# Packed 64x64 scores and a state per chunk in a gated linear attention, and its small steps moved from GpSimd to VectorE, in a fused encoder layer

## The chip, the cores and the metric

The kernel runs on one core of one Trainium2 chip and computes one whole layer for one sequence of 1024 frames and 1024 channels. The metric is the device time of one execution in microseconds (us). Each time is a median over runs of the compiled kernel; the profile is one more execution, taken apart by the chip's profiler. PE is TensorE (matmuls), DVE is VectorE, ACT is ScalarE, POOL is GpSimd, SP is SyncE, which issues the DMAs.

## What is computed

The layer is `x = LN1(alpha*x + gate1*m)`, `x = LN2(alpha*x + gate2*f)`; `f` is a feed-forward part of width 4096 and `m` mixes the tokens: `u @ w_in` is cut into heads, four heads of retention (with rotary positions) and four of gated linear attention (GLA), each normalized and gated, and `w_out` joins them. The change concerns the heads. The core of GLA, with chunks of 64 frames, keys of 64 and values of 128 channels a head, `b` being summed log gates:

```python
def step(state, inp):
    qi, ki, vi, lai = inp
    b = jnp.cumsum(lai, axis=1)
    decay = jnp.exp(-jnp.abs(b[:, :, None] - b[:, None, :]))
    A = jnp.einsum('bthd,bshd,btshd->bhts', qi, ki, decay)
    o = jnp.einsum('bhts,bshe->bthe', A, vi)
    o = o + jnp.einsum('bthd,bhde->bthe', qi * jnp.exp(b), state)
    b_last = b[:, -1]
    new_state = jnp.exp(b_last)[..., None] * state + jnp.einsum(
        'bshd,bshe->bhde', ki * jnp.exp(b_last[:, None] - b), vi)
    return new_state, o
```

Inside a chunk the decay differs for each channel and is symmetric in t and s, so A is not one matrix product.

## The kernel before

**Projections.** A product in float32 is made of three in fp32r: each operand is split into a high part, a cast on ScalarE, and a low part, source minus high part (`split`, L205 and L206; the low part goes to GpSimd unless the call names an engine), and `mm3` (L211 to L213) multiplies high by high, high by low and low by high. The contraction over 1024 channels runs in 8 blocks of 128, the frames in two halves `h` of 512. `load_w` brings a block of weights by DMA and splits it (`wh`, `wl`); `take` keeps one or two of the next weights loaded ahead. `modulate` makes the normalized input `u` and its parts `uh`, `ul`. `feature_major` puts channels on partitions (queries and keys), `values` puts frames there.

**GLA.** `gla(blk, h)` is called four times, for two pairs of heads (`blk`) and two halves of the frames; two heads of 64 channels lie one above the other on 128 partitions. A level of size u (32, 16, 8, 4, 2, 1) covers those pairs (t, s) of a chunk that lie in the two halves of one block of 2u frames: there |b_t - b_s| is a sum of two differences to the block's middle, and the scores are one product of decayed queries and keys. For each level GpSimd forms the differences `E` (L562, L563), ScalarE their exponentials (L564), VectorE the products `qe` and `ke` (L566, L567), TensorE the scores (L544, 128 frames by 128 frames for each of 2 heads and 4 blocks of frames; the profile shows each such matmul as two), and VectorE lays them over the sum `am` under the level's mask (`overlay`, L552). Two sets come ahead of the levels: the first chunk of each 128 frames against the second (`kB`, `qB`, copied under a mask, L554), and the diagonal (`k`, `q`, laid over under the identity).

**State.** It steps over 128 frames, so GpSimd makes `qI`, `kI` and `dt` (L576, L577, L580), which carry the first chunk's decay. TensorE transposes `kI` (L583) and forms the updates `up` (L593), VectorE makes the states one after another (L598, L600), TensorE reads them (L611) and adds the scores times the values (L617), and the heads are normalized (L621 to L626).

**Retention.** `retention_qk` turns the projections by the rotary tables: three products on VectorE (L647 to L649), their sum `t1` and the scaled queries `qd` on GpSimd (L650, L654); `retention` begins with scores at L663.

**Beside it.** `ada_sum` (L236, L238) sums the blocks of the conditioning vector's weights into `acc` on VectorE, and `load_out` splits the output weights (L800, `ol` on both engines).

**The order of work.** The program names its steps in the order of L751 to L786; the tile framework's scheduler then puts each engine's instructions into one order, by its own estimates of when operands and buffers are ready. Each engine works its row in order. Around the change:

```python
d = gla_decays(0, 0)
gla_qk(1)
ada(ada_row(2560, g1[1]))
gla(0, 0, gv0, *d)
d = gla_decays(0, 1)
gv1 = values(("gv", 1))
```

Of the kernel before, what the change touches and what calls it, by code (L numbers as in the profile page):

```python
# [16 lines left out]
P = 128  # L17
# [24 lines left out]
C_M64 = C_QD + 512  # L42
C_LV = C_M64 + 128
LEVELS = (32, 16, 8, 4, 2, 1)
C_KD = C_LV + 128 * len(LEVELS)
# [6 lines left out]
def shape_constants():  # L52
# [27 lines left out]
def layer_kernel(ctx: ExitStack, tc, x, c, w_ada, b_ada, w_in, ret_norm_w, gla_gate_w, gla_gate_b,  # L80
# [269 lines left out]
    def load_w(ranges, kk):  # L350
# [3 lines left out]
        for k in range(0, NK, kk):  # L354
# [6 lines left out]
            split(w, th, tl)  # L361
# [152 lines left out]
    def gla_decays(blk, h):  # L514
# [11 lines left out]
        G.tensor_tensor(out=ek.rearrange("p (n u) -> p n u", u=CHUNK),  # L526
# [7 lines left out]
    def gla(blk, h, gv, q, k, b, eb, qB, kB):  # L534
        am = [S(n="am"), S(n="am")]

        def scores(ka, qa, put):

            heads = [slice(64 * hd, 64 * hd + 64) for hd in range(2)]
            tiles = [slice(j * P, (j + 1) * P) for j in range(4)]  # L540
# [7 lines left out]
        def cmask(o):  # L548
            return table(o).unsqueeze(1).broadcast_to([P, 4, P])

        def overlay(o):
            return lambda a, ps: V.copy_predicated(out=a, mask=cmask(o).bitcast(U32), data=ps)  # L552

        scores(kB, qB, lambda a, ps: V.tensor_tensor(out=a, in0=ps, in1=cmask(C_M64), op=ALU.mult))  # L554
        scores(k, q, overlay(C_ID))
        for n, u in enumerate(LEVELS):
# [5 lines left out]
            G.tensor_tensor(out=ev[:, :, :u], in0=ref, in1=bv[:, :, :u], op=ALU.subtract)  # L562
            G.tensor_tensor(out=ev[:, :, u:], in0=bv[:, :, u:], in1=ref, op=ALU.subtract)  # L563
# [4 lines left out]
            scores(ke, qe, overlay(C_LV + P * n))  # L568


        eb4 = eb.rearrange("p (j c u) -> p j c u", c=2, u=CHUNK)
        qI, kI = S(n="qI"), S(n="kI")
        for src, dst, c0 in ((qB, qI, 0), (kB, kI, 1)):
            s4 = src.rearrange("p (j c u) -> p j c u", c=2, u=CHUNK)
            d4 = dst.rearrange("p (j c u) -> p j c u", c=2, u=CHUNK)
            G.tensor_copy(out=d4[:, :, c0, :], in_=s4[:, :, c0, :])  # L576
            G.tensor_tensor(out=d4[:, :, 1 - c0, :], in0=s4[:, :, 1 - c0, :],  # L577
                            in1=eb4[:, :, c0, CHUNK - 1:CHUNK].broadcast_to([P, 4, CHUNK]), op=ALU.mult)
        dt = small(4, "gdt", bufs=4)
        G.tensor_tensor(out=dt, in0=eb4[:, :, 0, CHUNK - 1], in1=eb4[:, :, 1, CHUNK - 1], op=ALU.mult)  # L580
        kp = mxt()
        for j in range(4):
            T.transpose(out=kp[:, j * P:(j + 1) * P], in_=kI[:, j * P:(j + 1) * P], identity=ident)  # L583
# [11 lines left out]
        states = S((P, 4, P), n="states")  # L595
        for j in steps:
            if before[j] is None:
                V.tensor_copy(out=states[:, j, :], in_=up[:, j, :])  # L598
            else:
                V.scalar_tensor_tensor(out=states[:, j, :], in0=before[j], scalar=dt[:, j:j + 1], in1=up[:, j, :],  # L600
                                       op0=ALU.mult, op1=ALU.add)
            before.append(states[:, j, :])
# [3 lines left out]
        with_state = [j for j in range(4) if before[j] is not None]  # L606
# [33 lines left out]
    def retention_qk(hd):  # L640
        res = [[], []]
        for key in ("rq", "rk"):
            pss = feature_major((key, hd))
            for h, ps in enumerate(pss):
# [5 lines left out]
                G.tensor_tensor(out=t1, in0=t1, in1=t2, op=ALU.add)  # L650
# [627 lines left out]
```

## Time and profile before

| | |
|---|---|
| Median of 3 runs | 1276.38 us (1275.5 to 1276.91) |
| The profiled execution: time | 1275.61 us |
| its span in the profile | 1273.8 us, 18210 instructions |
| PE busy | 1187.6 us, 93% |
| DVE busy | 965.2 us, 76% |
| ACT busy | 496.4 us, 39% |
| POOL busy | 301.0 us, 24% |

The span runs from the first to the last instruction; 1.8 us of the execution's time lie outside it. A busy share is a mean over stages that differ: the rows further down are taken by stretches. 0 to 128 us are the conditioning, the first norm and the first projections; 128 to 352 us hold GLA with the projections around it; up to 512 us run retention, the gates and the beginning of the output projection; then follow the rest of it and the feed-forward part. The granted clock is TensorE's, as a share of 2.4 GHz.

### The profile page before, as it was taken

Reading aid. Unit: us, or ns where it says so; the run is one execution under the profiler, and the core shown is the slowest. Engines: PE = TensorE matmul, PEld = TensorE weight load, DVE = VectorE, ACT = ScalarE, POOL = GpSimd, SP = SyncE. Lnnn points to the kernel's source line nnn. Section 1 sums busy time; section 2 is a strip of 40 time slices with the busy share of each in tenths; the row PEclk is TensorE's granted clock in tenths of the full one; section 3 lists DMA queues with packets and bytes.
Section 4 is the critical chain, followed back from the end, with each engine's and each line's share of the span. In section 5 each row is a group of like instructions: output and inputs, shape, how many; then the busy total and the mean of one; then the engine's idle time right before and its main releaser. Section 6 shows DMA issues by size and latency. Waiting matters only on the chain. (4 is left out here: it accounts for less than half of the span.)

```text
span 1273.8 us, 18210 instructions
## 1 busy us (share of the span) xinstructions
PE 1187.6 (93%) x6491; PEld 993.7 (78%) x6491; DVE 965.2 (76%) x1778; ACT 496.4 (39%) x879; POOL 301.0 (24%) x253
## 2 busy tenths in 40 slices
PE   4899899879899989999998999999999999999995
PEld 1588789667887979988886887888887788888784
DVE  6884876798757585379889978876657786897996
ACT  4424332122121323223475446665655443441222
POOL 1333442463324423000000000000002222242336
PEclk9899989889999999999999999999999999999998
DMA  9685220100011032227124768676464455458632
GB/s 313 207 269 200 83 59 5 38 25 26 9 50 34 21 105 65 77 77 246 53 93 149 245 203 300 232 248 207 149 220 164 142 190 186 134 192 284 233 124 100
DMA packets 124124, 183.31 MB, mean 144 GB/s; under 512 B 12337, under 2 KB 52482, under 8 KB 124034
## 3 DMA queue, kind: packets, MB, share of 16 engines
q1 hardware_dynamic: 124034, 182.16, 43.0%
q8 instruction: 51, 0.84, 0.3%
q14 instruction: 39, 0.32, 0.1%
HBM read 137.02 MB, written 45.09 MB: 143 GB/s over the span
## 5 line engine op out<-in xcount | busy, mean ns | idle before, releaser
L211 PE MATMUL pj<-wh,uh 128*128 128x256 f32 (+1 forms) x512 | 146.5, 287 | 0.3 <-ACT wh L205 0.3
L212 PE MATMUL pj<-wl,uh 128*128 128x256 f32 (+1 forms) x512 | 145.9, 285 | 0.3 <-POOL wl L206 0.3
L213 PE MATMUL pj<-wh,ul 128*128 128x256 f32 (+1 forms) x512 | 146.1, 286 | 0.0
L206 POOL TENSOR_TENSOR al<-rh,ah 128x512 fp32r<-128x512 f32 x17 | 26.7, 1571 | 468.0 <-ACT w1h L205 399.4
L206 POOL TENSOR_TENSOR wl<-st,wh 128x512 fp32r<-128x512 f32 (+1 forms) x60 | 78.2, 1320 | 190.3 <-ACT wh L205 118.9
L211 PE MATMUL pj<-uhp,w1h 128*128 128x512 f32 x256 | 100.2, 393 | 2.0 <-ACT w1h L205 1.1
L211 PE MATMUL pj<-bh,ah 128*128 128x512 f32 x256 | 99.8, 391 | 1.5 <-DVE qv L181 0.8
L212 PE MATMUL pj<-ulp,w1h 128*128 128x512 f32 x256 | 100.0, 391 | 0.0
L213 PE MATMUL pj<-uhp,w1l 128*128 128x512 f32 x256 | 99.9, 391 | 0.0
L212 PE MATMUL pj<-bl,ah 128*128 128x512 f32 x256 | 99.6, 389 | 0.0
L213 PE MATMUL pj<-bh,al 128*128 128x512 f32 x256 | 99.6, 389 | 0.0
L211 PEld LDWEIGHTS pj<-wh,uh 128*128 128x128 f32 x512 | 98.0, 192 | 1.3 <-ACT wh L205 0.7
L212 PEld LDWEIGHTS pj<-wl,uh 128*128 128x128 f32 x512 | 98.2, 192 | 0.9 <-POOL wl L206 0.5
L213 PEld LDWEIGHTS pj<-wh,ul 128*128 128x128 f32 x512 | 98.2, 192 | 0.4 <-issue 0.2
L211 PE MATMUL mx<-uhp,w1h 128*128 128x512 f32 x192 | 75.1, 392 | 2.7 <-ACT w1h L205 2.7
L211 PE MATMUL mx<-bh,ah 128*128 128x512 f32 x192 | 75.4, 394 | 2.1 <-ACT bh L205 1.2
L212 PE MATMUL mx<-bl,ah 128*128 128x512 f32 x192 | 75.6, 394 | 1.1 <-POOL bl L206 0.9
L213 PE MATMUL mx<-bh,al 128*128 128x512 f32 x192 | 75.5, 393 | 0.0
L213 PE MATMUL mx<-uhp,w1l 128*128 128x512 f32 x192 | 75.3, 393 | 0.0
L212 PE MATMUL mx<-ulp,w1h 128*128 128x512 f32 x192 | 75.3, 392 | 0.0
L212 PE MATMUL pj<-ul,wh 128*128 128x512 f32 x176 | 71.1, 406 | 4.3 <-DVE ul L206 2.6
L211 PE MATMUL pj<-uh,wh 128*128 128x512 f32 x176 | 72.0, 411 | 2.7 <-ACT uh L205 2.7
(266 smaller groups left out, 3014.5 us busy)
## 6 DMA issues: line engine op xcount, KB each, us to landing
raw<-in_w_ff SPq DMA_DIRECT2D x140, 256.0 KB, 4.2
ada<-in_w_ada SPq DMA_DIRECT2D x96, 256.0 KB, 5.4
rh<-hid SPq DMA_DIRECT2D x84, 256.0 KB, 3.7
hid<-c SPq DMA_DIRECT2D x54, 256.0 KB, 2.3
st<-in_w_in SPq DMA_DIRECT2D x52, 256.0 KB, 3.0
hid<-m SPq DMA_DIRECT2D x30, 256.0 KB, 2.2
hid<-kl SPq DMA_DIRECT2D x28, 256.0 KB, 3.1
hid<-kh SPq DMA_DIRECT2D x28, 256.0 KB, 2.7
```

Source lines behind the costliest of these rows:

```text
L206: (lo_eng or G).tensor_tensor(out=lo, in0=src, in1=hi.bitcast(F32), op=ALU.subtract)
L211: T.matmul(ps, lhsT=lh, rhs=rh, start=first, stop=False, skip_group_check=partial)
L212: T.matmul(ps, lhsT=lh, rhs=rl, start=False, stop=False, skip_group_check=partial)
L213: T.matmul(ps, lhsT=ll, rhs=rh, start=False, stop=last, skip_group_check=partial)
```

## The change

It has three parts. **Scores:** queries meet keys of their own chunk alone, as blocks of 64 by 64 that lie on four quarters of the PE array (two heads as row halves, two chunks as column halves), so `am` is half as wide, each mask has 64 columns, and the set of `qB` against `kB` is gone; the diagonal set is copied whole by ScalarE ahead of the levels. **State:** it steps over 64 frames, 8 (or 7) steps a call, with the last column of each chunk's `eb` as its decay; `qI`, `kI` and `dt` are gone; updates, state reads and the products of `am` and values are cut into more and smaller matmuls. **Engines:** whatever GpSimd computed in projections and mixing (`E`, `ek`, `wl`, half of `ul` and of `ol`, the rotary sum and `qd`) is written on VectorE. Lines of the program after the change are lower by one up to `gla` and differ a little within it (scores L549, overlay L556, `E` L565 and L566, `qe` and `ke` L569 and L570, `acc` L237, low part L205).

```diff
 modulate:
-        split(u, uh[k][h], ul[k][h], lo_eng=(V, G)[h])
+        split(u, uh[k][h], ul[k][h], lo_eng=V)
 load_w:
-            split(w, th, tl)
+            split(w, th, tl, lo_eng=V)
 gla_decays:
-        G.tensor_tensor(out=ek.rearrange("p (n u) -> p n u", u=CHUNK),
+        V.tensor_tensor(out=ek.rearrange("p (n u) -> p n u", u=CHUNK),
...
 gla:
-        am = [S(n="am"), S(n="am")]
+        am = S((P, 2, 4, CHUNK), n="am")
+        rows = [slice(CHUNK * i, CHUNK * i + CHUNK) for i in range(2)]
...
             pss = [mxt(), mxt()]
-            for o in tiles:
+            for j in range(4):
                 for hd in range(2):
-                    T.matmul(pss[hd][:, o], lhsT=ka[heads[hd], o], rhs=qa[heads[hd], o], start=True, stop=True)
+                    for ch in range(2):
+                        o = cols(2 * j + ch)
+                        T.matmul(pss[hd][rows[ch], cols(j)], lhsT=ka[rows[hd], o], rhs=qa[rows[hd], o], start=True,
+                                 stop=True)
             for hd in range(2):
-                put(am[hd].rearrange("p (j t) -> p j t", t=P), pss[hd].rearrange("p (j t) -> p j t", t=P))
+                put(am[:, hd], pss[hd][:, :4 * CHUNK].rearrange("p (j t) -> p j t", t=CHUNK))
...
-        scores(kB, qB, lambda a, ps: V.tensor_tensor(out=a, in0=ps, in1=cmask(C_M64), op=ALU.mult))
-        scores(k, q, overlay(C_ID))
+        scores(k, q, lambda a, ps: A.copy(out=a, in_=ps))
...
-            G.tensor_tensor(out=ev[:, :, :u], in0=ref, in1=bv[:, :, :u], op=ALU.subtract)
-            G.tensor_tensor(out=ev[:, :, u:], in0=bv[:, :, u:], in1=ref, op=ALU.subtract)
+            V.tensor_tensor(out=ev[:, :, :u], in0=ref, in1=bv[:, :, :u], op=ALU.subtract)
+            V.tensor_tensor(out=ev[:, :, u:], in0=bv[:, :, u:], in1=ref, op=ALU.subtract)
...
-        steps = range(4 if h == 0 else 3)
+        steps = range(8 if h == 0 else 7)
...
-        up = mxt((P, 4, P))
-        for j in steps:
-            vt = gv[2 * h + j // 2][:, j % 2, :]
+        up = [mxt((P, 4, P)), mxt((P, 4, P))]
+        for n in steps:
+            j, ch = n // 2, n % 2
             for hd in range(2):
-                T.matmul(up[64 * hd:64 * hd + 64, j, :], lhsT=kt[:, j * P + 64 * hd:j * P + 64 * hd + 64],
-                         rhs=vt[:, hd * P:(hd + 1) * P], start=True, stop=True)
+                T.matmul(up[ch][rows[hd], j, :], lhsT=kt[rows[ch], j * P + CHUNK * hd:j * P + CHUNK * hd + CHUNK],
+                         rhs=ve(j, hd, ch), start=True, stop=True)
...
-        for j in with_state:
-            o = slice(j * P, (j + 1) * P)
+        for n in with_state:
             for hd in range(2):
-                r = slice(64 * hd, 64 * hd + 64)
-                T.matmul(op[hd][:, j, :], lhsT=qI[r, o], rhs=before[j][r, :], start=j == with_state[0], stop=False,
-                         skip_group_check=True)
+                T.matmul(op[hd][rows[n % 2], n // 2, :], lhsT=qB[rows[hd], cols(n)], rhs=before[n][rows[hd], :],
+                         start=n in with_state[:2], stop=False, skip_group_check=True)
         for hd in range(2):
             for j in range(4):
-                o = slice(j * P, (j + 1) * P)
-                vt = gv[2 * h + j // 2][:, j % 2, :]
-                T.matmul(op[hd][:, j, :], lhsT=am[hd][:, o], rhs=vt[:, hd * P:(hd + 1) * P], start=False, stop=j == 3,
-                         skip_group_check=True)
+                for t in range(0, CHUNK, 32):
+                    for ch in range(2):
+                        T.matmul(op[hd][CHUNK * ch + t:CHUNK * ch + t + 32, j, :], lhsT=am[rows[ch], hd, j, t:t + 32],
+                                 rhs=ve(j, hd, ch), start=False, stop=j == 3, skip_group_check=True)
 retention_qk:
-                G.tensor_tensor(out=t1, in0=t1, in1=t2, op=ALU.add)
+                V.tensor_tensor(out=t1, in0=t1, in1=t2, op=ALU.add)
...
 load_out:
-                split(w, oh[k][q], ol[k][q], lo_eng=(G, V)[q])
+                split(w, oh[k][q], ol[k][q], lo_eng=V)
```

`qd` is written with V in place of G in the same way. The scheduler puts the work of the rest into other places than before; three show how.

**First place: PE, in the first call of gla(), between the scores of its first two levels.** `mx_1313`, `mx_1314` (`mx_1308`, `mx_1309` after) are the scores of level 32, `pj` a projection. Before:

```order
L544 MATMUL mx_1313<-qe_1309,ke_1310 128x128
L544 MATMUL mx_1314<-qe_1309,ke_1310 128x128
L544 MATMUL mx_1333<-qe_1329,ke_1330 128x128
L544 MATMUL mx_1334<-qe_1329,ke_1330 128x128
...
L212 MATMUL pj_1528<-wl_1150,uh_278 128x256
L213 MATMUL pj_1528<-wh_1149,ul_279 128x256
```

After:

```order
L549 MATMUL mx_1308<-qe_1304,ke_1305 64x64 x2
L549 MATMUL mx_1309<-qe_1304,ke_1305 64x64 x2
L212 MATMUL pj_1609<-wh_1161,ul_622 128x256
L210 MATMUL pj_1609<-wh_1161,uh_627 128x256
L211 MATMUL pj_1609<-wl_1162,uh_627 128x256
L212 MATMUL pj_1609<-wh_1161,ul_628 128x256
...
L549 MATMUL mx_1336<-qe_1332,ke_1333 64x64 x2
L549 MATMUL mx_1337<-qe_1332,ke_1333 64x64 x2
```

Before, the scores of the next level follow at once; after, 18 matmuls of a projection stand between the two levels. From the first to the last score matmul of the four calls there are 65, 65, 31 and 36 projection matmuls in the row before, and 129, 129, 68 and 96 after.

**Second place: DVE, in the same call, the same two levels.** `acc` belongs to the conditioning. Before:

```order
L566 TENSOR_TENSOR qe_1309<-gqk_694,E_1305 128x512
L567 TENSOR_TENSOR ke_1310<-gqk_778,E_1305 128x512
L238 SCALAR_TENSOR_TENSOR acc_2708<-ada_2698,keep,acc_2708 128x512
L566 TENSOR_TENSOR qe_1329<-gqk_694,E_1325 128x512
L567 TENSOR_TENSOR ke_1330<-gqk_778,E_1325 128x512
L238 SCALAR_TENSOR_TENSOR acc_2708<-ada_2700,keep,acc_2708 128x512
L552 COPY_PREDICATED am_1279<-cst_77,mx_1313 128x512
L552 COPY_PREDICATED am_1280<-cst_77,mx_1314 128x512
```

After:

```order
L569 TENSOR_TENSOR qe_1332<-gqk_694,E_1328 128x512
L570 TENSOR_TENSOR ke_1333<-gqk_778,E_1328 128x512
L565 TENSOR_TENSOR E_1356<-b_1108 128x32x8
L566 TENSOR_TENSOR E_1356<-b_1108 128x32x8
L237 SCALAR_TENSOR_TENSOR acc_2951<-ada_2943,keep,acc_2951 128x512
L556 COPY_PREDICATED am_1279<-cst_77,mx_1336 128x256
L556 COPY_PREDICATED am_1279<-cst_77,mx_1337 128x256
L569 TENSOR_TENSOR qe_1360<-gqk_694,E_1356 128x512
```

The two halves of the next level's `E` now stand behind `ke`, and the overlays are half as wide.

**Third place: DVE, behind the last level of the first call,** where the heads' norm is made (L172 to L174 are steps of the reciprocal root, `go` the normalized output) and the next call's decays begin. Before, and then after:

```order
L173 SCALAR_TENSOR_TENSOR rt_386_1498<-ry_385_1497 128x4
L174 TENSOR_TENSOR rt_386_1498<-rt_386_1498,rv_384_1496 128x4
L175 SCALAR_TENSOR_TENSOR grs_1494<-rt_386_1498,ry_385_1497 128x4
L626 TENSOR_TENSOR go_1510<-mx_1455,grs_1494 128x512
L530 TENSOR_TENSOR qB_1524<-gqk_696,eb_1518 128x512
```

```order
L172 SCALAR_TENSOR_TENSOR rt_382_1579<-ry_381_1578 128x4
L205 TENSOR_TENSOR wl_2175<-st_2172,wh_2174 128x512
L173 TENSOR_TENSOR rt_382_1579<-rt_382_1579,rv_380_1577 128x4
L205 TENSOR_TENSOR wl_2181<-st_2178,wh_2180 128x512
L174 SCALAR_TENSOR_TENSOR grs_1575<-rt_382_1579,ry_381_1578 128x4
L205 TENSOR_TENSOR wl_2760<-st_2757,wh_2759 128x512
L622 TENSOR_TENSOR go_1591<-mx_1504,grs_1575 128x512
L525 TENSOR_TENSOR ek_1602<-b_1598 128x512
L529 TENSOR_TENSOR qB_1605<-gqk_696,eb_1599 128x512
```

The low parts `wl` of the next weights have come in among these small steps, and `ek` ahead of `qB`.

## Rows read from the trace of the kernel before

**Rows 1.** Windows: us, busy us and instructions by engine, granted clock, DMA share, GB/s
```profile
0.00:128.00 128.00, 103.17 (x514) 74.80 (x515) 88.64 (x147) 53.27 (x97) 40.50 (x39) 0.96 0.74 246
128.00:352.00 224.00, 194.18 (x1569) 172.49 (x1568) 173.04 (x341) 53.28 (x91) 95.77 (x101) 0.94 0.12 35
352.00:512.00 160.00, 150.26 (x1072) 139.32 (x1072) 104.89 (x249) 42.34 (x73) 57.66 (x40) 1.00 0.20 57
```

**Rows 2.** Waits of PE, 128 to 352 us: total us, times, longest
```profile
PE mx L544 <- DVE ke L567: 24.8, 17, 8.2
```

**Rows 3.** Windows of the four bodies of gla(), their sum (102.5 us)
```profile
sum 102.50, PE 77.49 PEld 66.81 DVE 94.79 ACT 19.05 POOL 67.01; mean PE 19.37 PEld 16.70 DVE 23.70 ACT 4.76 POOL 16.75
```

**Rows 4.** Timeline, 266 to 285 us: start, us, engine, line, operation
```profile
...
267.72 1.59 POOL L654 TENSOR_TENSOR qd<-t,cst 128x512 f32<-128x512 f32 x1
268.20 1.66 DVE L648 TENSOR_TENSOR t<-p,rope 64x512 f32<-64x512 f32 x1
...
269.88 0.68 DVE L649 TENSOR_TENSOR t<-p,rope 64x512 f32<-64x512 f32 x1
...
```

**Rows 5.** Groups of DVE, 128 to 352 us: count, busy us, mean ns, idle before
```profile
L552 DVE COPY_PREDICATED am<-cst,mx 128x512 f32<-128x512 uint32 x48 | 31.7, 724 | 2.4 <-PE mx L544 2.2
L566 DVE TENSOR_TENSOR qe<-gqk,E 128x512 f32<-128x512 f32 x24 | 19.9, 831 | 4.2 <-ACT E L564 4.2
L567 DVE TENSOR_TENSOR ke<-gqk,E 128x512 f32<-128x512 f32 x24 | 19.1, 797 | 0.0
L238 DVE SCALAR_TENSOR_TENSOR acc<-ada,keep,acc 128x512 f32<-128x512 f32 x14 | 13.5, 967 | 0.1
L648 DVE TENSOR_TENSOR t<-p,rope 64x512 f32<-64x512 f32 x8 | 11.4, 1420 | 0.1
L647 DVE TENSOR_TENSOR t<-p,rope 128x512 f32<-128x512 f32 x8 | 9.8, 1228 | 0.9 <-ACT p L646 0.7
L649 DVE TENSOR_TENSOR t<-p,rope 64x512 f32<-64x512 f32 x8 | 8.5, 1059 | 0.1
...
L600 DVE SCALAR_TENSOR_TENSOR states<-states,gdt,mx 128x128 f32<-128x128 f32 x12 | 4.2, 348 | 1.7 <-PE mx L593 1.4
...
L531 DVE TENSOR_TENSOR kB<-gqk,ek 128x512 f32<-128x512 f32 x4 | 2.7, 685 | 0.0
```

**Rows 6.** Group of DVE, 352 to 512 us, a form of 256 columns
```profile
L736 DVE TENSOR_TENSOR mix<-sg,ro 128x256 f32<-128x256 f32 x6 | 2.3, 422 | 1.7 <-POOL ol L206 1.5
```

**Rows 7.** Groups of POOL, 128 to 352 us
```profile
L206 POOL TENSOR_TENSOR wl<-st,wh 128x512 fp32r<-128x512 f32 x17 | 23.1, 1374 | 58.4 <-ACT wh L205 47.8 <-PE pj L212 10.5
L562 POOL TENSOR_TENSOR E<-b 128x256 f32<-128x256 f32 x24 | 19.5, 814 | 12.6 <-DVE ke L567 9.8 <-DVE acc L238 2.7
...
L650 POOL TENSOR_TENSOR t<-t,t 128x512 f32<-128x512 f32 x8 | 12.6, 1574 | 8.8 <-DVE t L649 8.8
```

**Rows 8.** Timeline, 176 to 186 and 155.5 to 160.2 us
```profile
176.03 0.97 PEld L544 LDWEIGHTS mx<-qB,kB 64*128 64x128 f32 x16 [0.76 <-issue]
176.92 0.98 PEld L544 LDWEIGHTS mx<-gqk,gqk 64*128 64x128 f32 x16
...
178.24 0.28 PE L212 MATMUL pj<-wl,uh 128*128 128x256 f32 x1
178.36 0.28 PE L213 MATMUL pj<-wh,ul 128*128 128x256 f32 x1
...
155.58 1.09 PE L593 MATMUL mx<-v,kt 128*64 128x128 f32 x16
...
158.26 2.05 PE L617 MATMUL mx<-v,am 128*128 128x128 f32 x16
```

**Rows 9.** Waits of PE, 0 to 512 us
```profile
PE mx L663 <- POOL t L650: 3.1, 1, 3.1
...
PE pj L211 <- ACT uh L205: 2.7, 1, 2.7
PE pj L212 <- DVE ul L206: 2.6, 1, 2.6
```

More of the change, by code (lines that the diff above doesn't have):

```diff
@@ L41 @@
 C_QD = C_DEC + 512
[L42 to L43 removed]
+C_LV = C_QD + 512
 LEVELS = (32, 16, 8, 4, 2, 1)
[L45 removed]
+C_KD = C_LV + CHUNK * len(LEVELS)
 C_N = C_KD + 4
@@ L534, in gla, with cols @@
     def gla(blk, h, gv, q, k, b, eb, qB, kB):
-        am = [S(n="am"), S(n="am")]
+        am = S((P, 2, 4, CHUNK), n="am")
+        rows = [slice(CHUNK * i, CHUNK * i + CHUNK) for i in range(2)]
+        def cols(n):
+            return slice(CHUNK * n, CHUNK * n + CHUNK)
         def scores(ka, qa, put):
-            heads = [slice(64 * hd, 64 * hd + 64) for hd in range(2)]
-            tiles = [slice(j * P, (j + 1) * P) for j in range(4)]
             pss = [mxt(), mxt()]
-            for o in tiles:
+            for j in range(4):
                 for hd in range(2):
-                    T.matmul(pss[hd][:, o], lhsT=ka[heads[hd], o], rhs=qa[heads[hd], o], start=True, stop=True)
+                    for ch in range(2):
+                        o = cols(2 * j + ch)
+                        T.matmul(pss[hd][rows[ch], cols(j)], lhsT=ka[rows[hd], o], rhs=qa[rows[hd], o], start=True,
+                                 stop=True)
             for hd in range(2):
-                put(am[hd].rearrange("p (j t) -> p j t", t=P), pss[hd].rearrange("p (j t) -> p j t", t=P))
-        def cmask(o):
-            return table(o).unsqueeze(1).broadcast_to([P, 4, P])
+                put(am[:, hd], pss[hd][:, :4 * CHUNK].rearrange("p (j t) -> p j t", t=CHUNK))
         def overlay(o):
-            return lambda a, ps: V.copy_predicated(out=a, mask=cmask(o).bitcast(U32), data=ps)
-        scores(kB, qB, lambda a, ps: V.tensor_tensor(out=a, in0=ps, in1=cmask(C_M64), op=ALU.mult))
-        scores(k, q, overlay(C_ID))
+            m = table(o, CHUNK).unsqueeze(1).broadcast_to([P, 4, CHUNK]).bitcast(U32)
+            return lambda a, ps: V.copy_predicated(out=a, mask=m, data=ps)
+        scores(k, q, lambda a, ps: A.copy(out=a, in_=ps))
         for n, u in enumerate(LEVELS):
@@ L567, in gla @@
             V.tensor_tensor(out=ke, in0=k, in1=e, op=ALU.mult)
[L568 to L578, printed above, removed]
@@ L579, in gla, with ve @@
-        dt = small(4, "gdt", bufs=4)
-        G.tensor_tensor(out=dt, in0=eb4[:, :, 0, CHUNK - 1], in1=eb4[:, :, 1, CHUNK - 1], op=ALU.mult)
+            scores(ke, qe, overlay(C_LV + CHUNK * n))
         kp = mxt()
         for j in range(4):
-            T.transpose(out=kp[:, j * P:(j + 1) * P], in_=kI[:, j * P:(j + 1) * P], identity=ident)
+            T.transpose(out=kp[:, j * P:(j + 1) * P], in_=kB[:, j * P:(j + 1) * P], identity=ident)
         kt = S(n="kt")
         A.copy(out=kt, in_=kp)
-        steps = range(4 if h == 0 else 3)
+        def ve(j, hd, ch):
+            return gv[2 * h + j // 2][rows[ch], j % 2, hd * P:(hd + 1) * P]
@@ L603, in gla @@
+        states = [S((P, 4, P), n="states"), S((P, 4, P), n="states")]
+        for n in steps:
+            new, u = states[n // 4][:, n % 4, :], up[n % 2][:, n // 2, :]
+            if before[n] is None:
+                V.tensor_copy(out=new, in_=u)
+            else:
+                V.scalar_tensor_tensor(out=new, in0=before[n], scalar=eb[:, CHUNK * n + CHUNK - 1:CHUNK * n + CHUNK],
+                                       in1=u, op0=ALU.mult, op1=ALU.add)
+            before.append(new)
         gstate[blk] = before[-1]
@@ L604, in gla @@
         op = [mxt((P, 4, P)), mxt((P, 4, P))]
-        with_state = [j for j in range(4) if before[j] is not None]
-        for j in with_state:
-            o = slice(j * P, (j + 1) * P)
+        with_state = [n for n in range(8) if before[n] is not None]
+        for n in with_state:
             for hd in range(2):
-                r = slice(64 * hd, 64 * hd + 64)
-                T.matmul(op[hd][:, j, :], lhsT=qI[r, o], rhs=before[j][r, :], start=j == with_state[0], stop=False,
-                         skip_group_check=True)
+                T.matmul(op[hd][rows[n % 2], n // 2, :], lhsT=qB[rows[hd], cols(n)], rhs=before[n][rows[hd], :],
+                         start=n in with_state[:2], stop=False, skip_group_check=True)
@@ L653, in retention_qk @@
                     qd = S(n="qd")
-                    G.tensor_tensor(out=qd.rearrange("p (j t) -> p j t", t=P), in0=t1.rearrange("p (j t) -> p j t", t=P),
+                    V.tensor_tensor(out=qd.rearrange("p (j t) -> p j t", t=P), in0=t1.rearrange("p (j t) -> p j t", t=P),
                                     in1=table(C_QD + P * hd).unsqueeze(1).broadcast_to([P, 4, P]), op=ALU.mult)
```

11 lines of the change are left out of this document (2 added, 9 removed).

## The prediction

> **What bounds the kernel now.** The table of windows comes first [rows 1]: TensorE (PE) is busy 103 of 128, 194 of 224 and 150 of 160 us in the three stretches that the change touches, so it idles 25 + 30 + 10 us; behind 512 us the code is the same. The middle stretch holds the four calls of gla(). In the list of waits on PE there [rows 2], 24.8 of its 29.8 idle us stand behind ke (L567), which VectorE (DVE) writes. DVE is busy 173 of those 224 us, and in the four bodies of the calls (from the first to the last score matmul) 94.8 of 102.5 us while PE is busy 77.5 [rows 3]: the bodies are bound by DVE, the stretches between them by PE's projections. The granted clock is the other loss: 0.94 of 2.4 GHz in the mean of the stretch [rows 1], where PE stood for up to 8.2 us [rows 2]; part of the time it ran at 1.2.
>
> Why DVE is late is seen in the timeline [rows 4]: L648 at 268.20 takes 1.66 us and begins while GpSimd (POOL) works on qd from 267.72; L649 behind it, with as many columns, takes 0.68. One engine stands until the other is through. POOL has 95.8 us of work in the stretch [rows 1], and the change takes all of it away.
>
> **The change, part by part, at 128 to 352 us.**
>
> DVE loses its waits on POOL: L647, L648 and L649 mean 1228, 1420 and 1059 ns against 685 (kB's) free, 8 of each, 13.2 us; qe and ke 831 and 797, 24 of each, 6.2 us; acc 967, 14 of them, against at least 685, of which I take 3 us [rows 4, 5]. Together 22.4 us. It loses 16 instructions of 512 columns, the masked copies of the first set and the identity overlays, 11.0 us (ScalarE makes 8 copies of 256 columns instead; it is busy 53 of 224 us). The 48 overlays shrink from 512 to 256 columns: 724 ns becomes something between 362 (half) and 724. A 128x256 form on DVE takes 422 [rows 6] where 128x512 takes 685, so I take off 263 each, 12.6 us. Lost in all: 46.0 us.
>
> DVE gains POOL's instructions [rows 7], at 685 ns for 512 columns and 422 for 256: 48 halves of E (L562 and L563), 20.2 us; 17 wl, 11.6; 8 t, 5.5; 4 qd and 4 ek, 5.5; and 16 more state steps (28 for 12) at 348 ns [rows 5], 5.6. Gained: 48.4 us. **DVE's work stays as it is, near 175 us.** What moves is its place. From the bodies go the overlays' half, both first sets, the waits of qe, ke and acc, and some 8 us of L647 to L649 in the fourth: about 41 us; E and some t and qd come in, about 25. Most of wl, the state steps and ek come between the bodies, where DVE now idles 43 of 121 us. The wl rows stand among the small steps behind a call's last level (third place of the order above), none of them between two levels of the first two calls.
>
> PE: a set of scores is 16 passes (each fp32 matmul shows as two), two row halves of the array beside each other, and the next set's weight loads begin 0.89 us later, at 176.92 after 176.03 [rows 8]. 32 sets become 28, each of 32 passes of 64 columns on four quarters. If quarters overlap as row halves do, a set takes half of 0.89; if the two column quarters of a row half take turns, 0.89; if they don't get shorter either, 1.78. That column halves overlap shows: 16 passes of L593, 64 columns wide, take 1.09 us where 16 full ones of L617 take 2.05 [rows 8]. So I take 0.6, nearest the first: 28 x 0.6 = 16.8 against 32 x 0.89 = 28.5, **-11.7 us** of PE work (ends -16 and +21). The state updates, state reads and products with v get two to four times as many matmuls at the same columns per quarter: 0 by the same overlap. If only pairs overlap, twice the time: +0.9, +0.9 and +1.8 us a call, about +14 us over four calls, the end kept for the range.
>
> The Trainium skill speaks against this part: "TensorEngine Tiling (Array Packing)", section Restrictions and Gotchas, says that different row tiles can't access the same PSUM bank simultaneously. L617's new form does that: both row halves add into one bank, op[hd], in different partitions. By the rule those products go in pairs, some 7 us of PE work more and a sum up to 7 us later. No row here shows two row halves on one bank.
>
> The order moves more than the durations do. Between the first and the last score matmul of the calls stand now 65, 65, 31 and 36 projection matmuls, after the change 129, 129, 68 and 96 (first place of the order above). That is 128 more of 256 columns at 0.12 us (starts 178.24 and 178.36 [rows 8]) and 97 of 512 at twice that: 15.4 + 23.3 = **38.7 us of PE work that comes to lie beside DVE's chain instead of behind it**, more than the 25 us that PE idles in the bodies. So PE fills there.
>
> What then ends the stretch: PE has 194.2 - 11.7 us, and less of it at half clock. A mean of 0.94 is 12% of 224 us at 1.2 GHz, 13 us of work; with the waits broken up I let 10 come back. 172 us remain, and DVE needs 175: neither can be filled wholly beside the other. At the share that PE has now (194.2/224 = 0.867) the stretch takes 199 us: **-25 us**. Ends: at a share of 0.95, 181 us (-43); with nothing gained from quarters and clock and a share of 0.9 from the order alone, 215 us (-9).
>
> **0 to 128 us.** Fifteen and eight wl and eight ul leave POOL (40.5 us with the rest [rows 1]) for DVE, at half the time each. PE's first projections wait 2.7 us behind uh and 2.6 behind ul [rows 9]; both come from DVE beside POOL's wl. These 5.3 us can go, but wl then stand in line between the ul, and the DMA engines, 74% busy [rows 1], set what comes behind. -2 us (-5 to +3).
>
> **352 to 512 us.** PE idles 10 us, 3.1 of them behind t (L650 on POOL, 1574 ns) [rows 7, 9]. DVE takes 40 instructions of 0.69 there, 27 us, beside 105 busy of 160, and loses waits of the same kind as above. -3 us (-9 to +5).
>
> Sum: -2 - 25 - 3 = -30 from the profiled execution's 1275.61 us, which stands 0.8 below the median of 1276.38: **1246 us**. Its own range is 1225 to 1257.
>
> **Rivals.**
>
> *DVE stays the bound.* Its sum is unchanged, so the levels could take as long as now, and the moved projections only find what the 16 us less of DVE work in the bodies leave. Against it: the new order puts some 18 projections of 256 columns into nearly every level. E's new place in DVE's line (second place of the order above) costs some 4 of the 16: -12 in all, 1264 us.
>
> *Quarters go in pairs.* For it: no row shows four quarters at work. PE has +10 us then (sets of 0.89, four fewer, -3.6, and +14) instead of -11.7, and in the filled bodies PE is the bound. Of the 22 us I let two thirds show: 1260 us.
>
> *DVE stands behind a weight split: slower.* POOL sat idle 58.4 us ahead of its 17 wl in this stretch, 47.8 of them behind the ScalarE cast wh and 10.5 behind PE [rows 7]. DVE works in order: a wl at its head keeps back qe, ke and the state steps, and PE with them. It decides when more than 30 of those 58 us show on DVE; with 45 it gives 1246 + 45 = 1291 us. Against it: the rows put wl behind the levels, and while the weight buffers are full PE has work.
>
> *It doesn't do what it says.* What leaves the bodies returns as waits for weights between them: 1275 us.
>
> **How the numbers follow.** Forecast 0.53, DVE bound 0.16, pairs 0.14, weight split 0.12, no effect 0.05. A measurement of this kernel can tell about 0.2% (2.5 us) from no change. Faster: 0.53 + 0.16 + 0.14 = 0.83; same 0.05; slower 0.12. The range takes the forecast's own ends and both lesser gains, 1225 to 1270, and leaves out the weight split and no effect.
>
> **What would show it.** Right: no POOL work from 10 to 512 us; L648 near 690 ns throughout; PE's wait behind ke under 12 us; a mean clock of 0.98 in the second stretch; sets of scores under 0.7 us; the first matmul of retention() some 25 us earlier. Wrong: overlays above 0.6 us; sets of 0.9 us or more; DVE idle behind the cast wh for over 10 us; a gain at 128 to 352 us that is given back behind 512.

## The result, and the profile after

The changed kernel takes **1245.42 us** (median of 4 runs, 1242.42 to 1247.72) against 1275.94 us before: ratio 0.9748, 95% interval 0.9731 to 0.9765. The forecast was 1246. Its profiled execution took 1245.99 us, its span 1244.2.

The windows below are cut at the first score matmul, at the first matmul of retention() and at the first transpose of the mixed heads; between these marks both kernels run the same projections. Before, and then after (us, busy us by engine, granted clock, DMA share, GB/s):

```profile
0.00:131.60 131.60, 106.41 (x525) 76.78 (x526) 90.07 (x150) 56.84 (x103) 42.25 (x41) 0.96 0.72 239
131.60:320.10 188.50, 163.49 (x1338) 143.25 (x1338) 149.39 (x274) 46.80 (x81) 85.55 (x94) 0.94 0.14 40
320.10:437.50 117.40, 109.84 (x735) 100.71 (x735) 78.93 (x208) 19.93 (x33) 43.69 (x30) 0.99 0.11 30
```

```profile
0.00:125.30 125.30, 104.86 (x527) 77.36 (x527) 91.49 (x179) 54.49 (x99) 0.76 (x8) 0.97 0.75 249
125.30:290.40 165.10, 152.47 (x2043) 127.06 (x2043) 132.79 (x321) 49.51 (x90) 0.00 (x0) 0.96 0.16 48
290.40:407.00 116.60, 109.89 (x734) 100.80 (x734) 89.90 (x266) 20.99 (x35) 0.00 (x0) 0.97 0.10 28
```

The time comes from 0 to 125 us (-6.3) and from GLA (-23.4); retention gives -0.8, what lies behind it +0.9. The last has two parts. From the first to the last transpose of the mixed heads, where GpSimd made 8 ol and 8 wl before, the change takes 103.0 us for 109.4. Behind the last transpose both kernels run the same instructions (before, then after):

```profile
546.90:1273.80 726.90, 705.04 (x3095) 574.33 (x3093) 589.06 (x1023) 341.71 (x610) 107.04 (x73) 0.99 0.54 183
```

```profile
510.00:1244.20 734.20, 709.25 (x3095) 576.62 (x3093) 590.32 (x1023) 341.38 (x610) 107.87 (x73) 0.99 0.54 181
```

There the change takes 7.3 us more: PE is busy 4.2 us longer, with 20 us at the lower clock level for 12, and idle 3.1 longer. Why is not shown; in the profiles of the study this stretch takes 726 to 734 us.

In GLA PE is busy 11.0 us less and idle 12.4 less (25.0 to 12.6). VectorE does about the same work, in the whole program 962.8 us for 965.2. The waits of PE from 126 to 325 us [rows 2]:

```profile
PE mx L691 <- DVE rs L662: 6.4, 1, 6.4
PE mx L549 <- DVE ke L570: 6.3, 11, 2.4
```

ke fell from 24.8 to 6.3 us; rs, at the start of retention, rose from 4.4. The four bodies of gla() together [rows 3]:

```profile
sum 110.00, PE 98.08 PEld 82.40 DVE 99.37 ACT 34.40 POOL 0.00; mean PE 24.52 PEld 20.60 DVE 24.84 ACT 8.60 POOL 0.00
```

They got longer, 110.0 for 102.5 us, and hold 98 us of PE work for 77. VectorE's groups, 126 to 325 us [rows 5, 7]:

```profile
L556 DVE COPY_PREDICATED am<-cst,mx 128x256 f32<-128x256 uint32 x48 | 18.5, 440 | 7.4 <-PE mx L549 7.4
L569 DVE TENSOR_TENSOR qe<-gqk,E 128x512 f32<-128x512 f32 x24 | 16.4, 685 | 1.0 <-ACT E L567 0.8
L570 DVE TENSOR_TENSOR ke<-gqk,E 128x512 f32<-128x512 f32 x24 | 16.4, 684 | 0.0
L205 DVE TENSOR_TENSOR wl<-st,wh 128x512 fp32r<-128x512 f32 x17 | 11.6, 688 | 2.3 <-ACT wh L204 2.2
L237 DVE SCALAR_TENSOR_TENSOR acc<-ada,keep,acc 128x512 f32<-128x512 f32 x14 | 10.4, 746 | 0.1
L565 DVE TENSOR_TENSOR E<-b 128x256 f32<-128x256 f32 x24 | 10.1, 419 | 0.0
...
L644 DVE TENSOR_TENSOR t<-p,rope 64x512 f32<-64x512 f32 x8 | 5.5, 686 | 0.1
```

The forms are back at their undisturbed duration: 686 ns where the rotary product took 1420. Last, PE's groups that the packing changes, before (128 to 352 us) and after (126 to 325 us) [rows 8]:

```profile
L544 PE MATMUL mx<-qe,ke 64*128 64x128 f32 x384 | 33.0, 320 | 24.9 <-DVE ke L567 24.8
L617 PE MATMUL mx<-v,am 128*128 128x128 f32 x64 | 8.2, 281 | 0.0
L544 PE MATMUL mx<-gqk,gqk 64*128 64x128 f32 x64 | 5.6, 275 | 0.0
L611 PE MATMUL mx<-states,qI 64*128 64x128 f32 x56 | 4.9, 297 | 0.0
L544 PE MATMUL mx<-qB,kB 64*128 64x128 f32 x64 | 4.6, 284 | 0.4 <-DVE kB L531 0.4
L593 PE MATMUL mx<-v,kt 128*64 128x128 f32 x56 | 3.9, 280 | 0.0
```

```profile
L549 PE MATMUL mx<-qe,ke 64*64 64x64 f32 x768 | 17.1, 227 | 6.7 <-DVE ke L570 6.3
L607 PE MATMUL mx<-states,qB 64*64 64x128 f32 x120 | 9.7, 314 | 0.0
L613 PE MATMUL mx<-v,am 64*32 64x128 f32 x256 | 7.8, 270 | 0.0
L589 PE MATMUL mx<-v,kt 64*64 64x128 f32 x120 | 5.3, 311 | 0.7 <-ACT kt L577 0.7
L549 PE MATMUL mx<-gqk,gqk 64*64 64x64 f32 x112 | 4.4, 226 | 1.0 <-DVE go L622 1.0
```

The last row lacks the first of its four sets, which lies ahead of 126 us; with it they take 5.1 us. A set of the levels takes 17.1 / 24 = 0.71 us, so four quarters do work beside each other (with two at a time it is 1.0, as an experiment below shows); am times v has four times the passes in 7.8 us for 8.2, and in the trace they start four at a time, within 20 ns.

### The profile page after: what moved, and what is told of

It is laid out like the page before. It is cut to its first block, busy times and chain, and to the rows that moved or that the text cites. A ratio compares the mean times of both kernels' runs of the same rounds, so it can differ in the third digit from the quotient of the medians.

```text
span 1244.2 us, 19474 instructions
## 1 busy us (share of the span) xinstructions
PE 1178.3 (95%) x7195; PEld 980.3 (79%) x7195; DVE 962.8 (77%) x1930; ACT 496.6 (40%) x887; POOL 108.6 (9%) x81
## 5 line engine op out<-in xcount | busy, mean ns | idle before, releaser
L205 POOL TENSOR_TENSOR al<-rh,ah 128x512 fp32r<-128x512 f32 x17 | 26.6, 1567 | 923.1 <-PE pj L212 861.1
L205 DVE TENSOR_TENSOR w1l<-raw,w1h 128x512 fp32r<-128x512 f32 x80 | 54.7, 686 | 25.9 <-ACT w1h L204 17.1
```

The lines of the kernel that those rows point to most:

```text
L205: (lo_eng or G).tensor_tensor(out=lo, in0=src, in1=hi.bitcast(F32), op=ALU.subtract)
```

## The experiments

"The change" is the changed kernel. An effect in us is the difference of two ratios times 1276; the change's own ratio is good to 0.0017 either way, and the others' to 0.0015 to 0.0033, so effects under 3 to 5 us are not told apart. Stretches are from one profile each, cut at the marks above; "rest" holds the stretch behind the last transpose, which differs by up to 8 us between profiles though nothing is edited there.

| run | median us | ratio (95%) | to first score | GLA | retention | rest |
|---|---|---|---|---|---|---|
| before | 1275.94 | 1 | 131.6 | 188.5 | 117.4 | 836.3 |
| the change | 1245.42 | 0.9748 (0.9731 to 0.9765) | 125.3 | 165.1 | 116.6 | 837.2 |
| engines only | 1252.23 | 0.9821 (0.9789 to 0.9854) | 127.9 | 177.7 | 115.6 | 828.5 |
| packing only | 1271.16 | 0.9953 (0.9938 to 0.9969) | 130.6 | 179.0 | 118.9 | 840.9 |
| low parts on POOL | 1264.29 | 0.9898 (0.9879 to 0.9917) | 132.0 | 172.4 | 118.9 | 840.0 |
| rotary sums on POOL | 1252.38 | 0.9807 (0.9789 to 0.9824) | 125.8 | 168.6 | 123.9 | 831.9 |
| E on POOL | 1237.48 | 0.9694 (0.9674 to 0.9714) | 125.0 | 166.4 | 108.3 | 833.7 |
| order held | 1252.79 | 0.9818 (0.9798 to 0.9839) | 125.4 | 182.1 | 108.6 | 834.5 |
| order held, fourth call | 1246.33 | 0.9762 (0.9743 to 0.9780) | 128.0 | 174.8 | 108.6 | 834.8 |
| E on POOL, order forced, fourth held | 1246.02 | 0.9769 (0.9742 to 0.9795) | 125.2 | 176.2 | 108.5 | 831.0 |
| E on POOL, order forced | 1241.31 | 0.9715 (0.9692 to 0.9738) | 124.7 | 166.0 | 114.3 | 832.1 |
| E on POOL, go on ScalarE | 1240.88 | 0.9704 (0.9671 to 0.9737) | 125.1 | 164.7 | 112.8 | 834.3 |
| scores in pairs | 1249.09 | 0.9773 (0.9748 to 0.9799) | 125.8 | 171.5 | 117.5 | 835.5 |
| one overlay a set | 1231.03 | 0.9636 (0.9612 to 0.9661) | 124.6 | 156.7 | 117.3 | 830.5 |

### The two halves of the change

Engines only: the kernel before with G turned into V wherever the change does it.

```diff
-            split(w, th, tl)
+            split(w, th, tl, lo_eng=V)
...
-            G.tensor_tensor(out=ev[:, :, :u], in0=ref, in1=bv[:, :, :u], op=ALU.subtract)
+            V.tensor_tensor(out=ev[:, :, :u], in0=ref, in1=bv[:, :, :u], op=ALU.subtract)
...
```

> The kernel before with the engine moves alone (E, ek, wl, half of ul and ol, the rotary sum and qd on VectorE; old 128x128 scores, old masks, old state; qI, kI and dt stay on GpSimd). VectorE then has 173 - 22.4 (waits on GpSimd) + 42.8 (moved steps, without the state steps) = 193 us of work where the change has about 175; the order puts 110, 127, 61 and 95 projections into the four bodies (65, 65, 31, 36 before). My theory (VectorE's chain sets the bodies, the order fills PE beside it): the bodies get longer, about 28 us each for 22.6 to 24.3, the stretches between them shorter by the projections that moved; 5 to 15 us faster than before, about 1266 us, PE idle behind ke still over 10 us. Rival (the engine moves are the whole gain, the packing is hidden): 1245 to 1250 us.

Packing only: the change with the same lines turned back.

> The changed kernel with all arithmetic back on GpSimd (E, ek, wl, half of ul and ol, rotary sum, qd); packed scores and a state per chunk stay. The order puts 76, 76, 34 and 44 projections into the bodies, little more than before. My theory: VectorE loses 23.6 us (half overlays, first sets) and gains 5.6 in state steps, nearly all of the loss inside the bodies, and PE loses 11.7 us; the bodies shrink by 12 to 18 us in all: 1258 to 1264 us. VectorE's forms again vary (rotary products, qe, ke up to 1.3 to 1.7 us). Rival (GpSimd's E, 0.8 us a half, is the bound of a level once VectorE is faster): less than 6 us gained, over 1270 us.

Engines only gave 22.8 us, more than I expected and near the rival's size; the bodies did get longer, 122.9 us together, and GLA gained 10.8 us as the theory had it, but the stretches around it gained 13 more (3.7, 1.8 and 7.8 in the rest). Packing only gave 6 us, the rival's size: GLA gained 9.5 us and lost some of it behind. The rival's reason shows too. In the group of qe (130 to 430 us of that run) VectorE waits 12.7 us for E, where it waited 4.2 before and 1.0 in the change:

```profile
L569 DVE TENSOR_TENSOR qe<-gqk,E 128x512 f32<-128x512 f32 x24 | 20.7, 861 | 12.7 <-ACT E L567 12.7
```

On top of the moved engines the packing is worth 0.0073, 9 us. The two halves nearly add up to the whole (22.8 + 6.0 for 32.2 by these ratios).

### Which of the moved steps pays

Low parts, rotary sums and E went back to GpSimd one at a time, each from the change.

```diff
-            split(w, th, tl, lo_eng=V)
+            split(w, th, tl)
...
```

> The changed kernel with the low parts (wl, half of ul, half of ol) back on GpSimd. Theory: what I sized at -2 us ahead of the first score and measured at -6.3 is these low parts; then the first score comes at 130 to 131.5 us (125.3 in the change). In GLA VectorE loses 11.7 us of wl, most of it between the bodies, and runs into GpSimd's 1.4 us steps instead: within 3 us. In all 1247 to 1254 us. Rival (low parts are covered on either engine): 1243 to 1247 us, first score at 125 to 126.

```diff
-                V.tensor_tensor(out=t1, in0=t1, in1=t2, op=ALU.add)
+                G.tensor_tensor(out=t1, in0=t1, in1=t2, op=ALU.add)
...
```

> The changed kernel with the rotary sum t and qd back on GpSimd (12 and 6 instructions in retention, some in the fourth call). Theory: the rotary products on VectorE again take up to 1.3 to 1.7 us beside them instead of 0.69; that makes the fourth body and the start of retention later: 3 to 8 us slower than the change, 1248 to 1253 us. Rival (VectorE's sum is what counts: 24 fewer instructions of 0.69 us are worth as much as the waits): 1242 to 1247 us.

```diff
-            V.tensor_tensor(out=ev[:, :, :u], in0=ref, in1=bv[:, :, :u], op=ALU.subtract)
-            V.tensor_tensor(out=ev[:, :, u:], in0=bv[:, :, u:], in1=ref, op=ALU.subtract)
+            G.tensor_tensor(out=ev[:, :, :u], in0=ref, in1=bv[:, :, :u], op=ALU.subtract)
+            G.tensor_tensor(out=ev[:, :, u:], in0=bv[:, :, u:], in1=ref, op=ALU.subtract)
```

> The changed kernel with the level differences E alone back on GpSimd. VectorE loses 20 us of work and gets some 6 us of waits back; the order falls to 84, 67, 34 and 62 projections in the bodies (129, 129, 68, 96 in the change). If the order carries the gain (my theory): the bodies shorten, but 107 projections (12.6 + 15.4 us of PE work) come back between them: 5 to 15 us slower than the change, 1250 to 1260 us. If VectorE's work carries it (rival: VectorE stays the bound of the stretch): 10 us less of it, so as fast as the change or faster, 1237 to 1246 us.

The **low parts** cost 19 us on GpSimd, beyond both expectations: 6.7 us ahead of the first score, as expected there, 7.3 in GLA, 5 behind. Of the last, the stretch from the first to the last transpose alone takes 6.6 us more (109.6 for 103.0; 110.8 with packing only), so ol and wl on GpSimd cost there too. The order moved somewhat with them, to 114, 120, 66 and 96 projections in the bodies. What GLA loses is seen at 218 us of that run, in the timeline and in PE's waits from 132 to 305 us:

```profile
218.30 2.97 POOL L205 TENSOR_TENSOR wl<-st,wh 128x512 fp32r<-128x512 f32 x2 [1.68 <-ACT wh L204]
```

```profile
218.78 1.36 DVE L569 TENSOR_TENSOR qe<-gqk,E 128x512 f32<-128x512 f32 x1 [1.55 <-ACT E L567]
220.06 1.75 DVE L570 TENSOR_TENSOR ke<-gqk,E 128x512 f32<-128x512 f32 x1
```

```profile
PE mx L549 <- DVE ke L570: 16.5, 13, 4.0
```

Two wl run on GpSimd, and qe and ke, 0.69 us each without them, take 1.36 and 1.75; PE waits for ke. The windows of GLA and retention in that run give the price of one:

```profile
132.00:304.30 172.30, 152.54 (x2043) 127.52 (x2042) 137.20 (x303) 46.90 (x86) 23.79 (x17) 0.94 0.16 46
304.30:423.20 118.90, 112.23 (x734) 102.60 (x734) 88.50 (x254) 21.63 (x36) 15.93 (x12) 0.96 0.10 27
```

29 wl (17 + 12 on POOL) left VectorE, 29 x 0.688 = 20.0 us, and yet it is busy 225.7 us for 222.7 in the change: 23 us came back as waits, 0.79 us for each wl. (Busy time counts the overlap of neighbouring records once; by the sum of the durations it is 0.72.) So a wl costs VectorE about as much from GpSimd as on VectorE itself, and there it strikes whatever stands at the head of the row. The **rotary sums** cost 7 us, within the expectation. Their groups, 240 to 420 us:

```profile
L644 DVE TENSOR_TENSOR t<-p,rope 64x512 f32<-64x512 f32 x16 | 21.9, 1366 | 0.2
L643 DVE TENSOR_TENSOR t<-p,rope 128x512 f32<-128x512 f32 x16 | 14.7, 916 | 5.1 <-POOL t L646 2.9 <-ACT p L642 2.0
L645 DVE TENSOR_TENSOR t<-p,rope 64x512 f32<-64x512 f32 x16 | 12.9, 808 | 0.2
```

Against 686 ns each this is 16 x (0.68 + 0.23 + 0.12) = 16.5 us of waits for 24 moved steps of 0.69, 16.6 us: again no work is saved on VectorE.

**E** goes the other way: on GpSimd the kernel is 7 us faster than the change, the rival's case. Its windows:

```profile
125.00:291.50 166.50, 150.42 (x2044) 124.89 (x2043) 134.92 (x296) 47.68 (x91) 35.49 (x47) 0.96 0.16 46
291.50:399.80 108.30, 107.97 (x734) 99.11 (x735) 84.51 (x244) 20.58 (x35) 0.00 (x0) 1.00 0.12 33
```

VectorE is busy 219.4 us for 222.7, though 20.1 us of E are gone: 17 came back as waits, 0.35 us a half for 0.42 on VectorE (13 and 0.27 by the sum of the durations). GLA takes as long as in the change; the gain lies in retention, 108.3 us for 116.6, where PE idles 0.3 us for 6.7. Since the order moved with E (84, 67, 34 and 62 projections in the bodies), the engine's share and the order's are not told apart by this run. The other runs tell more of retention. Among the kernels with the rotary sums on VectorE it takes 108 to 109 us where 31 to 62 projections stand in the fourth body, 112.8 and 114.3 with 66 and 80, and 115.6 to 118.9 with 95 or 96: the gain there goes with the order.

### The order of the projections

Each projection matmul was tied, for its place in the row alone, behind the last score matmul of a set; the fourth call alone in the second run.

```diff
+            if ends:
+                n = min(6, done * 6 // room)
+                with tc.issue_after(ends[n].ins):
+                    T.matmul(ps, lhsT=l, rhs=r, start=a, stop=z, skip_group_check=partial)
+                done += 1
...
+    done, room = 0, 65
     gv1 = values(("gv", 1))
```

> The changed kernel with the order of the projections held: order-only dependencies let just 65, 65, 31 and 36 projection matmuls pass between the first and the last score matmul of the four calls, spread evenly over the levels, as many as before the change (129, 129, 68 and 96 in the change). Engines, operations and durations are the change's. My theory: 128 projections of 256 columns and 96 of 512, 37 us of PE work, come behind the bodies again; the bodies can shrink only by what PE held them up, at most 10 us: 20 to 28 us slower than the change, 1265 to 1273 us. Rival (the durations carry the gain, not the order): within 5 us of the change, 1245 to 1250 us.

> The changed kernel with the order held in the fourth call of gla() alone (36 projection matmuls of retention_qk(1) between its first and last score instead of 96, spread over the levels); the first three calls as in the change. Theory now: in the first three calls the new order is a gain (118.2 us from the first score to the fourth body, 133.1 with all four held), but in the fourth it uses up the projections that covered PE at the start of retention (wait of 6.4 us behind rs, clock 0.89; retention stretch 116.6 us, 108.6 with all held). Then the fourth call gets some 2 us longer and retention 8 us shorter: 1236 to 1241 us, with the first retention matmul at about 292 us. Rival (the shorter retention came from something that the hold of the first three calls left behind, such as the low parts made earlier on VectorE): 1244 to 1249 us.

The windows of GLA and retention with all four calls held:

```profile
125.40:307.50 182.10, 150.64 (x2043) 124.93 (x2042) 143.70 (x351) 50.04 (x90) 0.00 (x0) 0.95 0.14 42
307.50:416.10 108.60, 108.14 (x734) 99.19 (x734) 80.22 (x237) 21.08 (x35) 0.00 (x0) 1.00 0.12 32
```

In GLA the order is worth 17.0 us, somewhat under the theory; but 8.0 us of it are given back in retention, and the whole is 9 us, between theory and rival. The 17 us hold for E in VectorE's row: with E on GpSimd, 84, 67, 34 and 62 projections in the bodies went with a GLA of 166.4 us, no longer than the change's. The change's order lets all 96 projections of retention_qk(1) pass before the last levels of the fourth call; nothing is left to cover PE when retention begins, while VectorE still works off rotary products, and PE waits the 6.4 us for rs.

Holding the fourth call alone should then have kept both gains. It did not (0.9762, same as the change; the rival's time, but not its reason): retention took 108.6 us as expected, but the fourth call, from its first score to retention, 56.6 us in place of 46.9. PE's waits there, and the body's window, in this run and with all four held:

```profile
PE mx L558 <- DVE ke L580: 12.7, 4, 10.8
```

```profile
246.20:281.30 35.10, 18.17 (x262) 12.83 (x262) 31.40 (x61) 8.31 (x16) 0.00 (x0) 0.71 0.06 16
```

```profile
258.50:286.10 27.60, 16.59 (x262) 12.14 (x262) 24.28 (x49) 5.74 (x11) 0.00 (x0) 0.81 0.08 22
```

VectorE has 7 us more to do inside the body: 18 rotary steps of retention_qk(0) for 12, the call's own ek, qB and kB, and a go of the third call. With all calls held these had been done in the longer stretch ahead of it. What the order covers in one place it pushes into VectorE's row in another.

The same with E on GpSimd, each score tied behind the projections that stand ahead of it in the change; in the first of two runs with the fourth call held.

```diff
+        done += 3
+        for n in range(1, 7):
+            if sets and caps and caps[n] <= done < caps[n] + 3:
+                for m in sets[n]:
+                    tc.add_manual_dep(m.ins, i.ins.name, ...)
```

> E back on GpSimd, with the change's order forced in the first three calls (129, 129 and 69 projections in the bodies, spread over the levels) and the fourth held as before (31). If the order is worth as much here as in the change (theory): the first three calls take 118 us or less instead of 124.3 with E on GpSimd alone, since VectorE has less to do in them; the fourth and retention stay: 1228 to 1233 us, the fastest so far. Rival (with E on GpSimd the levels wait for GpSimd's 0.8 us halves, and filled bodies only get longer): 1236 to 1243 us.

> E back on GpSimd, the change's order forced in the first three calls, the fourth call left to the scheduler (80 projections in its body). The earlier run with the order forced and the fourth call held lost 12 us in the fourth call (54.6 us from its first score to retention, 42.2 with E on GpSimd alone) and gained 3 in the first three. Theory: without the hold the fourth call is back near 42 to 46 us, and the gain of the first three stays: 1233 to 1239 us, as fast as E on GpSimd alone (1237). Rival (the forced order itself pushes VectorE's rotary products into the fourth body, hold or not): 1242 to 1248 us.

The first is slower than theory and rival: the first three calls gain 2.8 us (121.5 for 124.3), and the fourth, held, loses 12 as above. The second lies between: 121.6 us, a fourth call of 44.4 as expected, and then retention gives 6.0 back (114.3 for 108.3); its interval overlaps that of E on GpSimd alone. The order is no gain that can be put on top of it. Nor does E on GpSimd shorten these calls: with as many projections in them, the first three take 118.2 us in the change.

### What the levels are bound by

Scores in pairs: one column half of the array after the other.

```diff
-            for j in range(4):
-                for hd in range(2):
-                    for ch in range(2):
+            for ch in range(2):
+                for j in range(4):
+                    for hd in range(2):
```

> The changed kernel with the score matmuls of a set issued one column half of the array after the other, so that only two quarters work beside each other. It prices PE's work in the levels: a set of 32 passes, 0.63 us in the change, should become 0.9 to 1.1 us, 28 sets, 8 to 13 us more PE work. If PE is the bound of the filled bodies: 1253 to 1258 us. If VectorE is, and PE has room: 1243 to 1248 us. If both are near full and neither covers the other wholly (theory): 1248 to 1253 us.

One overlay a set:

```diff
-            for hd in range(2):
+            for hd in range(2 if ka is k else 1):
                 put(am[:, hd], pss[hd][:, :4 * CHUNK].rearrange("p (j t) -> p j t", t=CHUNK))
```

> The changed kernel without the overlays of the second head (24 copies of 128x256 on VectorE, 0.44 us each, 10.6 us; the second head then keeps the scores of its diagonal set alone). It prices VectorE's work in the levels. The order has 112, 107, 56 and 96 projections in the bodies. If VectorE is the bound: 8 to 11 us faster than the change, 1234 to 1237 us. If PE is: 1243 to 1247 us. If both (theory): 1238 to 1242 us.

The pairs' group of scores (125 to 298 us) and the two runs' windows of GLA:

```profile
L549 PE MATMUL mx<-qe,ke 64*64 64x64 f32 x768 | 24.0, 228 | 3.9 <-DVE ke L570 3.9
```

```profile
125.80:297.30 171.50, 162.73 (x2043) 137.16 (x2043) 133.49 (x321) 49.49 (x91) 0.00 (x0) 0.94 0.16 46
```

```profile
124.60:281.20 156.60, 148.03 (x2043) 123.31 (x2043) 125.76 (x297) 48.95 (x90) 0.00 (x0) 0.98 0.17 50
```

10.2 us more of PE work cost 3 us, with intervals that overlap the change's; in GLA, by one profile, 6.4 us. 10.6 us less of VectorE work gave 14 us: 8.4 in GLA, with 17, 22, 12 and 0 projections fewer in the bodies and PE 4.4 us less busy at a clock of 0.98 for 0.96, and 6.7 in the rest, where nothing was edited and the cause is open. In GLA each price shows for more than half, as it would with both near full. By the whole time VectorE's row weighs more, but that the levels hang on it alone is not shown.

### A faster version

E on GpSimd, all else as in the change, has the lowest time of the kernels that compute the whole layer: 1237.48 us (the interval of its order forced overlaps). One more step was tried on it, go as ScalarE copies with a scale:

```diff
-            V.tensor_tensor(out=g, in0=op[hd], in1=rs.unsqueeze(2).broadcast_to([P, 4, P]), op=ALU.mult)
+            for j in range(4):
+                A.activation(g[:, j, :], op[hd][:, j, :], AF.Copy, scale=rs[:, j:j + 1])
```

> E back on GpSimd, and the last product of the heads' norm (go, 8 of 0.69 us on VectorE) as 32 ScalarE copies of 128x128 with a scale: 5.5 us off VectorE, on an engine that is busy a third of the time there. Theory (VectorE's work counts where the tails of a call stand ahead of the next call's first products): 1 to 4 us faster than E on GpSimd alone, 1233 to 1237 us. Rival (the tails are covered by PE's projections): 1237 to 1240 us.

It is no faster (0.9704 for 0.9694, 1240.88 us), near the rival's case: GLA gained 1.7 us and retention lost 4.5.

## Why the prediction was right, and where it was not

**The sum** was right, 1246 for 1245.4, but in part by luck. GLA's -25 came as -23.4. The stretch ahead gave -6.3 for -2, outside its ends of -5 to +3; retention and what follows up to the last transpose gave -0.8 and -6.4 for -3. Against them stand the 7.3 us behind the last transpose, which the sum has at nothing and the list of signs has as one of being wrong ("given back behind 512"). And the working behind the -25 was right by errors that cancel.

**VectorE's work** "stays as it is": 965.2 and 962.8 us in the whole program; waits gone, overlays 440 ns (461 by my term), POOL's steps at 688 and 419. Right, term by term.

**PE's work** was to fall by 11.7 (scores) and 10 (clock). The scores alone fell by 43.2 - 22.2 = 21.0 us: I priced the old sets at 0.89 us, a time between starts at full clock, and 24 of them were busy 33.0 / 24 = 1.38. Two of them, the second at the lower clock level:

```profile
151.14 1.16 PE L544 MATMUL mx<-qe,ke 64*128 64x128 f32 x16 [0.34 <-DVE ke L567]
...
184.17 2.08 PE L544 MATMUL mx<-qe,ke 64*128 64x128 f32 x16 [2.91 <-DVE ke L567]
```

The clock was 0.84 to 0.89 in three of the four bodies. Against it the smaller matmuls of the state cost 6.2 us (4.9 + 3.9 to 9.7 + 5.3), which I had put at 0: in three calls the state reads stand in groups of mostly 4 or 8 passes between projections, and in the fourth 31 of them stretch over 3.55 us beside VectorE's state steps. The same 576 projection matmuls, now cut up by the levels, are busy 104.0 us by their records for 99.0. And the clock gave back less: 0.96 for 0.94, not 0.98, as two of the bodies still run at 0.93. By the forecast's own working (12% of 188.5 us at the lower level, 8% of 165.1 after) that is an estimated 5 us of work for 10, and it is part of what the scores lost. All in all -11.0, not -21.7.

**PE's share** of the stretch I took as unchanged, 0.867; it rose to 152.47 / 165.10 = 0.92. With the order held it is 150.64 / 182.10 = 0.83, so the moved projections account for the rise. The step that failed is "at the share that PE has now": with PE's real work it gives 176 us, not 165.

**0 to 128 us.** The forecast was -2, because wl would stand between the ul. With the low parts on VectorE the first score came at 124.6 to 128.0 us, with them on GpSimd at 130.6 to 132.0: about -5. PE's wait of 2.6 us behind ul is 0.4 now. Of the 5.3 us of waits that the forecast took mostly back, 3.3 are gone (behind uh 1.6 us for 2.7).

**What I took for the cause.** I wrote that the order moves more than the durations. Shown is less: 17 us in GLA, where it is the largest part, but 9 in all. The largest part of the whole is the low parts, 19 us (not all of it theirs alone, as the order moved a little with them), which stand in my sum as a cost of 11.6 us of VectorE work, and in a rival as the way to get slower. That rival priced how long VectorE would stand behind the cast wh (up to 45 us); it stands 2.2. What it left out is the other side: how long VectorE stood behind GpSimd's wl, at the head of a level. The sum has these waits only as 6.2 us of VectorE work (qe and ke).

**The rivals.** "VectorE stays the bound" has some support for its premise in the missing overlays (8.4 us of GLA for 10.6), and the wrong time: its 1264 took VectorE's chain as no shorter than its work in the bodies. Pairs are excluded by the sets of 0.71 us, a little above the sign of 0.7; for the scores alone they cost 3 us by the ratios. "It doesn't do what it says" holds for retention, where the order gives 8 us back.

**The rule weighed there.** By "TensorEngine Tiling (Array Packing)" of the Trainium skill, section Restrictions and Gotchas, the products of am and v would go in pairs. The row says that they don't: 256 passes of a quarter's rows by 32 columns took 7.8 us for 64 whole ones in 8.2, starting four at a time, with both row halves adding into one bank, in different partitions. No run here has them in the same partitions.

## What to carry to other kernels

Ahead of moving a step from GpSimd to VectorE, count what it costs VectorE where it is: the lengthened forms beside it, against its own duration there. Here a 512-column step cost about the same either way and gained by no longer striking the chain, while the kernel with the 256-column halves of E left on GpSimd was 7 us faster, in retention, with the order that came with it. When a scheduler's new order fills one engine beside a chain, look for the stretch from which that cover was taken.

## What was not expected of the hardware

That GpSimd's step holds up VectorE by some third to half of its own length: 0.7 to 0.8 us per wl of 1.38, 0.7 per rotary step of 1.61, 0.3 to 0.35 per half of E of 0.8, while the overlays, which read PSUM, took 439 ns with wl on GpSimd as without. "SBUF — State Buffer" of the Trainium skill, section "SBUF: two separate sides", describes the pair of ports between the two engines as a lock that one holds for a whole instruction; the 1.36 and 1.75 us above agree with a lock. Also that halving the quarters at work, 32 passes in 1.0 us in place of 0.71, cost so little: 3 us in all, 6.4 in GLA, for 10 us of PE work.
